# A planned two-layer encoder kernel: library pauses counted for GpSimd, an early broadcast from xT, another order of steps in the feed-forward groups, and a last half stored in three cuts

## The chip, the cores and the metric

The kernel runs on one core of a Trainium2 chip. The time is the device time of one execution in microseconds; the profiled execution's span (first to last instruction) is given beside it. The engines are TensorE (PE, with PEld for its weight loads), VectorE (DVE), ScalarE (ACT), GpSimd (POOL) and SyncE (SP), which issues most of the loads.

## The reference

Two layers on x of 256 tokens by 1024, in float32. Each layer has three steps with a residual and a LayerNorm: half of a gated feed-forward, a mixer, and half of a second gated feed-forward. The mixer of layer 0 is a bidirectional chunked mLSTM, that of layer 1 is attention in a window of 128 tokens.

```python
def swiglu(x, w_in, w_out):                      # 1024 -> 2 x 2816 -> 1024
    gu = x @ w_in
    g, u = gu[..., :D_FF], gu[..., D_FF:]
    return (jax.nn.silu(g) * u) @ w_out

def reference(x, ...):
    for l in range(DEPTH):                       # DEPTH = 2
        x = layer_norm(ALPHA * x + 0.5 * swiglu(x, ffn_w_in[l, 0], ffn_w_out[l, 0]), ...)
        y = mlstm_mixer(x, ...) if l % 2 == 0 else window_attention(x, ...)
        x = layer_norm(ALPHA * x + y, ...)
        x = layer_norm(ALPHA * x + 0.5 * swiglu(x, ffn_w_in[l, 1], ffn_w_out[l, 1]), ...)
    return x
```

In the mLSTM mixer, q, k, v, an output gate o and the gates i and f come from x @ w_in. For each of four heads and both directions the scores q k^T are multiplied by weights exp(u_s - max) with a causal mask, applied to v and divided by their sum; the two directions are added, each head is normalised, scaled by norm_g, multiplied by sigmoid(o), and goes through w_out.

## The kernel before

**Numbers.** TensorE multiplies in a short float32 format. Each operand is split into a high part and the remainder, and each product is three matmuls (hi·hi, hi·lo, lo·hi; `mm3`, L691). For a block of weights, ScalarE casts the high part `w_hi` and VectorE subtracts to get `w_lo` (`split`, L652); one such block, 512 KB, is called a word here. The tokens are two halves of 128, t = 0 and 1; x stands transposed in the constant tiles `xT_hi` and `xT_lo` (128 x 8 x 256).

**Stages.** There are six: feed-forward, mLSTM, feed-forward, feed-forward, attention, feed-forward. The up-projections and the v part of the mLSTM's projection are made in groups of seven block products in place of eight (`strassen`, L904): P1, P2, S1, S2, S3, S4 and A22, each in two steps. The S products use sums of blocks of x, and some words are sums of blocks of weights: either VectorE adds two loaded words in place (`plus`, rows `b11<-b11,b12`), or a DMA on GpSimd's queue adds one block onto another as it lands (`bring`, L923). A22 takes the word b11 after such an adding DMA (`fourth_word`, L945). In a feed-forward group, T0 and T1 are the transposes of the hidden values of a half, and d is one row of the down-projection (12 matmuls). The order of a group is a string: FIRST, FULL, SHUT and OPEN (L54 to 57) for the feed-forward, used 1, 11, 4 and 3 times, and MIXES for the mLSTM. In the mLSTM, H0 to H3 make a head's scores and weights, M0 to M3 the mix with v, the division and the head's normalisation.

**The planner.** Nothing is issued where it is written. `Book` records every instruction, `cost` (L333) gives each a duration, `latest` (L396) a due time counted back from TensorE's order, and `sequence` (L424) simulates the five engines and picks for each the next instruction among those due first. TensorE's order alone is the written one. `emit` then issues all of them, so that every instruction of the kernel has line 600 (611 after the change). The table FEW (L63) holds how long a small DMA on GpSimd's queue is counted to take to land, by the tile that it fills.

**GpSimd's part.** It raises to a power (`TENSOR_TENSOR` with `mhalf`: the reciprocal root of a LayerNorm, `rs`, and of a head's normalisation, `hrs`, L804 and L1373), copies a row to all partitions (`partition_broadcast`, which is a bare ISA row in the program's order), masks (`affine_select`), and issues the adding DMAs. In the mLSTM, `scans` (L1246) makes the gates' running sums and maxima; `most` (128 x 2 x 256) takes the maxima by two small DMAs, and `weights(h)` (L1288) broadcasts head h's row of it into `wt`, ScalarE takes the exponentials, and GpSimd masks them. A broadcast of `gl` into `most` (L1248) is overwritten later: its result is not used.

**The end.** In the last stage's half t = 1 the first step of the LayerNorm (mean and gain) runs on pieces of 512, 256 and 256 columns, the second (power and bias) and the store on the two `cuts` of 512 (`Norm.finish`, L789 to 813).

## Time and profile before

| | |
|---|---|
| three runs | 910.62, 910.65, 911.04 us |
| the profiled execution | 910.77 us |
| its span | 909.1 us |
| mean granted TensorE clock | 0.996 |
| DMA | 220.07 MB, mean 242 GB/s |
| the chain that ended last | PE 73%, issue 10%, DVE 8%, DMA 4%, ACT 3%, POOL 2% |

How to read it: busy time is given for each engine in microseconds and as a share of the span. A row of a timeline is one instruction, or several in a row of one kind (x2), with its start, its duration, the engine, the tiles that it writes and reads, and in brackets how long its engine stood idle before it and which instruction ended that. In the program's order a tile's name carries a number (`b11_1424`), in the timeline it doesn't (`b`).

### The profile page before, as it was taken

The numbers are of one execution on the slowest core, as the hardware profiler recorded it, in microseconds if no ns is written. First come the engines' busy times: TensorE is split into PE (matmuls) and PEld (weight loads), VectorE is DVE, ScalarE is ACT, GpSimd is POOL, SyncE is SP. The second block draws the span as 40 slices with busy tenths as digits, with TensorE's granted clock in tenths as the row PEclk, the third lists the DMA queues.
The fourth block names the chain that finished last, engine by engine and source line by source line (L and its number), as shares of the span: only waits on it lengthen the run. The fifth ranks groups of instructions, "written<-read, shape, count | busy, mean of one in ns | idle before, by whom it ended". The sixth has DMA issues, their size and how long they took to land.

```text
span 909.1 us, 12673 instructions
## 1 busy us (share of the span) xinstructions
PE 892.3 (98%) x4375; PEld 743.6 (82%) x4375; DVE 823.9 (91%) x1008; ACT 656.5 (72%) x927; POOL 169.8 (19%) x201
## 2 busy tenths in 40 slices
PE   8999999999989999999999999999999999999996
PEld 7888888887978888888888888888898788888885
DVE  7999998798987999999889999997789899999974
ACT  6767677685866887776768767775689888677651
POOL 0111221213321212122021212140132231112100
PEclk9999999999999999999999999999999999999999
DMA  9998999937585999999985899999533778999931
GB/s 320 379 305 215 333 300 283 286 75 197 181 277 145 229 236 330 266 267 307 344 238 144 215 319 299 269 268 365 181 123 109 182 188 217 318 256 280 319 71 46
DMA packets 107744, 220.07 MB, mean 242 GB/s; under 512 B 7288, under 2 KB 23696, under 8 KB 107680
## 3 DMA queue, kind: packets, MB, share of 16 engines
q1 hardware_dynamic: 84000, 174.09, 54.6%
q0 software_dynamic: 23680, 45.18, 29.1%
q8 instruction: 34, 0.56, 0.2%
q14 instruction: 30, 0.25, 0.1%
HBM read 218.18 MB, written 1.05 MB: 241 GB/s over the span
## 4 chain that ended last, share of the span: by engine, by line
PE 73%; issue 10%; DVE 8%; DMA 4%; ACT 3%; POOL 2%; DVEq 0%; SPq 0%; POOLq 0%; ACTq 0%
PE pw L600 45%; PE py L600 28%; DVE w_lo L600 3%; DMA b<-in_ffn_w_in_dram 2%; ACT w_hi L600 1%; POOL b L600 1%; DMA b<-in_ml_w_in_dram 1%; DMA raw<-in_ffn_w_in_dram 1%; DVE e L600 0%; DVE pv L600 0%; DMA raw<-in_ffn_w_out_dram 0%; DVE x L600 0%; DVE h L600 0%; ACT sc L600 0%; POOL rs L600 0%
## 5 line engine op out<-in xcount | busy, mean ns | idle before, releaser
L600 ACT CAST w_hi<-b 128x1024 fp32r<-128x1024 f32 x280 | 292.0, 1053 | 107.8 <-PE py L600 48.3
L600 DVE TENSOR_TENSOR w_lo<-b,w_hi 128x1024 fp32r<-128x1024 f32 x280 | 334.4, 1221 | 11.5 <-ACT w_hi L600 10.9
L600 PE MATMUL pw<-w_hi,S 128*128 128x512 f32 x640 | 205.4, 390 | 0.1
L600 DVE TENSOR_TENSOR w_lo<-raw,w_hi 128x1024 fp32r<-128x1024 f32 (+1 forms) x150 | 179.1, 1213 | 11.7 <-ACT w_hi L600 10.9
L600 POOL DMA_DIRECT2D b<-in_ffn_w_in_dram x80 | 97.1, 1225 | 493.5 <-DVE b L600 205.8
L600 ACT CAST w_hi<-raw 128x1024 fp32r<-128x1024 f32 (+1 forms) x150 | 155.0, 1041 | 40.8 <-PE py L600 20.5
L600 PE MATMUL pw<-w_hi,xT_hi 128*128 128x512 f32 (+1 forms) x400 | 157.8, 396 | 1.9 <-ACT w_hi L600 1.2
L600 PE MATMUL pw<-w_hi,xT_lo 128*128 128x512 f32 (+1 forms) x400 | 154.7, 388 | 0.2 <-DVE xT_lo L600 0.2
L600 PE MATMUL pw<-w_lo,xT_hi 128*128 128x512 f32 (+1 forms) x400 | 153.9, 388 | 0.8 <-DVE w_lo L600 0.8
L600 PEld LDWEIGHTS pw<-w_hi,S 128*128 128x128 f32 x640 | 120.1, 188 | 25.8 <-ACT S L600 0.5
L600 PE MATMUL pw<-w_lo,S 128*128 128x512 f32 x320 | 124.5, 389 | 0.0
L600 PE MATMUL py<-w_hi,h_hi 128*128 128x512 f32 x317 | 124.4, 393 | 0.0
L600 PE MATMUL py<-w_hi,h_lo 128*128 128x512 f32 x317 | 123.6, 390 | 0.0
L600 PE MATMUL py<-w_lo,h_hi 128*128 128x512 f32 x317 | 123.4, 389 | 0.0
L600 DVE TENSOR_TENSOR b<-b,b 128x1024 f32<-128x1024 f32 x74 | 90.4, 1223 | 0.8
L600 PEld LDWEIGHTS pw<-w_hi,xT_lo 128*128 128x128 f32 x400 | 75.3, 188 | 17.4 <-DVE xT_lo L600 2.0
L600 PEld LDWEIGHTS pw<-w_hi,xT_hi 128*128 128x128 f32 x400 | 75.3, 189 | 17.3 <-ACT w_hi L600 1.9
L600 PEld LDWEIGHTS pw<-w_lo,xT_hi 128*128 128x128 f32 x400 | 75.4, 189 | 15.3 <-DVE w_lo L600 1.5
L600 PEld LDWEIGHTS pw<-w_lo,S 128*128 128x128 f32 x320 | 60.1, 188 | 12.2
L600 PEld LDWEIGHTS py<-w_hi,h_lo 128*128 128x128 f32 x317 | 59.5, 188 | 12.6
L600 PEld LDWEIGHTS py<-w_lo,h_hi 128*128 128x128 f32 x317 | 59.6, 188 | 12.0
L600 PEld LDWEIGHTS py<-w_hi,h_hi 128*128 128x128 f32 x317 | 59.5, 188 | 12.0
(211 smaller groups left out, 1134.5 us busy)
## 6 DMA issues: line engine op xcount, KB each, us to landing
b<-in_ffn_w_in_dram SPq DMA_DIRECT2D x152, 512.0 KB, 8.0
raw<-in_ffn_w_out_dram SPq DMA_DIRECT2D x88, 512.0 KB, 8.6
b<-in_ffn_w_in_dram POOLq DMA_DIRECT2D x80, 512.0 KB, 9.2
raw<-in_ffn_w_in_dram SPq DMA_DIRECT2D x36, 256.0 KB, 6.6
raw<-in_ml_w_in_dram SPq DMA_DIRECT2D x16, 512.0 KB, 6.0
raw<-in_at_w_in_dram SPq DMA_DIRECT2D x12, 512.0 KB, 8.9
b<-in_ml_w_in_dram SPq DMA_DIRECT2D x8, 512.0 KB, 6.6
raw<-in_ml_w_out_dram SPq DMA_DIRECT2D x8, 512.0 KB, 3.5
```

The costliest lines, as they stand in the source:

```text
L600: getattr(engines[s.engine], s.name)(*[real(x) for x in s.args], **{k: real(x) for k, x in s.kw.items()})
```

## The change

It has five parts. The planner keeps which of two libraries GpSimd has loaded ("B" for `partition_broadcast`, "A" for the rest, with `affine_select` and DMAs belonging to either) and counts 7200 ns (SWITCH) when the next instruction needs the other one. Some of its numbers for GpSimd change: FEW for `most`, and the costs of the broadcast, the select and the power of more than one column. A new broadcast of 8 columns of `xT` into a small tile `ready`, which nothing reads, stands ahead of the gates, and the broadcast of `gl` is gone. In FULL, SHUT and OPEN single steps stand elsewhere. The last half's final cut of 512 columns becomes two of 256, each with its scaling and its store.

```diff
-FULL = "P1*2 d T1 P2*2 S1*2 S2*2 d S3*2 S4*2 d A22*2 d T0"
-SHUT = "T1 P1*2 d P2*2 S1*2 S2*2 d*2 S3*2 S4*2 A22*2 T0"
-OPEN = "a*1 P1*2 a*3 p P2*2 x1 b*1 x2 S1 b*1 S1 S2 x3 x4 b*1 S2 b*1 S4*2 t S3*2 d A22*2 T0"
+FULL = "P1*2 d T1 P2*2 S1*2 S2*2 d S3*2 d S4*2 A22*2 d T0"
+SHUT = "T1 P1*2 d P2 d P2 S1*2 S2*2 d S3*2 S4*2 A22*2 T0"
+OPEN = "a*1 P1*2 a*3 p P2*2 x1 b*1 x2 S1 b*1 S1 S2 x3 x4 b*1 S2 S4 b*1 S4 t S3*2 d A22*2 T0"
-FEW = {"most": 8500.0, "few": 9500.0}
+FEW = {"most": 3200.0, "few": 9500.0}
+SWITCH = 7200.0
+    def library(self):
+        return {"partition_broadcast": "B", "affine_select": "", "dma_start": ""}.get(self.name, "A")
-            s.takes = {"tensor_tensor": 1500.0, "partition_broadcast": 1100.0, "iota": 600.0,
-                       "affine_select": 1600.0}.get(s.name, n * 0.93 + 100.0)
+            s.takes = {"tensor_tensor": 1500.0, "partition_broadcast": 900.0, "iota": 600.0,
+                       "affine_select": 900.0}.get(s.name, n * 0.93 + 100.0)
+            if s.name == "tensor_tensor" and n > 1:
+                s.takes = 1000.0
+        library = "A"
-                    if e == "POOL" and "accum_op" not in s.kw:
+                    if e == "POOL" and "accum_op" not in s.kw and s.name != "partition_broadcast":
                         t = max(t, s.due - EARLY)
+                    if e == "POOL" and s.library() not in ("", library):
+                        t = max(t, free[e] + SWITCH)
+            if e == "POOL":
+                library = s.library() or library
-            cuts = [slice(0, 512), slice(512, D)] if self.last else [A]
+            cuts = [slice(0, 512), slice(512, 768), slice(768, D)] if self.parted else [slice(0, 512), slice(512, D)] if self.last else [A]
         def gates():
+            nc.gpsimd.partition_broadcast(small("ready", (128, 8)), xT[0][0:1, 7, 248:256].bitcast(F32))
         def scans():
             nc.scalar.copy(gl, pg[64:128])
-            nc.gpsimd.partition_broadcast(most[:, 0], gl[0:1])
```

GpSimd's order at the start of the mLSTM stage before: `rs` is the power of the stage's first LayerNorm, `b11` are the two words of A22 that the adding DMAs complete, and `most` the broadcast's target. A bare ISA row names no tile.

```order
L600 DMA few_74<-in_ml_norm_g_dram 128x8x1
L600 TENSOR_TENSOR rs_1789<-rs_1789,few_74 128x1
L600 DMA b11_1407<-in_ml_w_in_dram 128x2x512
L600 ISA
L600 ISA most_1900<-gl_1896 128x256
L600 DMA b11_1424<-in_ml_w_in_dram 128x2x512
L600 DMA most_1900<-scan_1915 4x256 x2
```

The same place after:

```order
L611 DMA few_74<-in_ml_norm_g_dram 128x8x1
L611 TENSOR_TENSOR rs_1789<-rs_1789,few_74 128x1
L611 ISA
L611 ISA ready_1872<-xT_hi_71 128x8
L611 DMA b11_1405<-in_ml_w_in_dram 128x2x512
L611 DMA b11_1424<-in_ml_w_in_dram 128x2x512
L611 DMA most_2052<-scan_1915 4x256 x2
```

The bare ISA row and a broadcast moved from between the two adding DMAs to a place ahead of both, and the broadcast reads `xT_hi` in place of `gl`.

GpSimd's order at the heads of the mLSTM before: `wt_2355` and `wt_2426` are the weights of heads 2 and 3, the first `hrs` is the power of head 0, the second that of head 1.

```order
L600 ISA wt_2355<-most_1900 128x256 x2
L600 AFFINE_SELECT wt_2355<-wt_2355 128x256 x2
L600 ISA wt_2426<-most_1900 128x256 x2
L600 ISA
L600 TENSOR_TENSOR hrs_2437<-hrs_2437,few_74 128x2
L600 AFFINE_SELECT wt_2426<-wt_2426 128x256 x2
L600 TENSOR_TENSOR hrs_2601<-hrs_2601,few_74 128x2
```

And after, where `wt_2343` and `wt_2398` are the weights of heads 2 and 3:

```order
L611 ISA wt_2343<-most_2052 128x256 x2
L611 AFFINE_SELECT wt_2343<-wt_2343 128x256
L611 ISA wt_2398<-most_2052 128x256
L611 AFFINE_SELECT wt_2343<-wt_2343 128x256
L611 ISA wt_2398<-most_2052 128x256
L611 AFFINE_SELECT wt_2398<-wt_2398 128x256 x2
L611 ISA
L611 TENSOR_TENSOR hrs_2426<-hrs_2426,few_74 128x2
L611 TENSOR_TENSOR hrs_2576<-hrs_2576,few_74 128x2
```

The bare ISA row and head 0's power now stand behind head 3's selects.

VectorE's order there before: `den` is a mix's divisor, `h0` and `h1` are the two token halves of the heads' output, `hmv` and `hrs` a head's mean and power, and `wt` are head 2's weights, which become TensorE's operand `a`.

```order
L600 TENSOR_TENSOR den_2495<-den_2495,ecol_2072 128x4
L600 RECIPROCAL den_2495<-den_2495 128x4
L600 TENSOR_SCALAR h0_2397<-h0_2397,hmv_2433,hrs_2437 128x256
L600 TENSOR_TENSOR wt_2355<-pw_2500,wt_2355 128x2x256
L600 TENSOR_TENSOR wt_2355<-pw_2500,wt_2355 128x2x128
L600 TENSOR_SCALAR h1_2402<-h1_2402,hmv_2433,hrs_2437 128x256
L600 SCALAR_TENSOR_TENSOR h0_2397<-py_2450,den_2495,h0_2397 128x256
L600 TENSOR_TENSOR a_lo_2535<-wt_2355,a_hi_2527 128x768
```

And after; head 0's scaling by `hrs_2426` comes eleven rows behind the last one shown:

```order
L611 TENSOR_TENSOR den_2458<-den_2458,ecol_2073 128x4
L611 RECIPROCAL den_2458<-den_2458 128x4
L611 TENSOR_TENSOR wt_2343<-pw_2502,wt_2343 128x2x256
L611 TENSOR_TENSOR wt_2343<-pw_2502,wt_2343 128x2x128
L611 SCALAR_TENSOR_TENSOR h0_2385<-py_2454,den_2458,h0_2385 128x256
L611 BN_STATS hst_2530<-h0_2385 128x6
L611 BN_AGGR hmv_2534<-hst_2530 128x2
L611 TENSOR_TENSOR a_lo_2538<-wt_2343,a_hi_2526 128x768
```

The scaling that needs head 0's power has moved from ahead of head 2's weights to behind the weights and divisors of heads 2 and 3.

VectorE's order in the last group but one of the last feed-forward stage before: `e2` and `e5` become the hidden values of the two halves, whose transposes T0 and T1 follow, `b11` rows with two `b` are sums of words, and `w_lo` are remainders.

```order
L600 TENSOR_TENSOR e2_8152<-pw_8098,e2_8152 128x512
L600 TENSOR_TENSOR e2_8152<-e1_8109,e2_8152 128x512
L600 TENSOR_TENSOR b11_7946<-b11_7946,b12_8086 128x1024
L600 TENSOR_TENSOR w_lo_8247<-b21_8076,w_hi_8213 128x1024
L600 TENSOR_TENSOR w_lo_8255<-b11_7931,w_hi_8225 128x1024
L600 TENSOR_TENSOR b11_7931<-b11_7931,b22_8114 128x1024
L600 TENSOR_TENSOR e5_8126<-g1_8268,e5_8126 128x512
L600 TENSOR_TENSOR w_lo_8280<-b11_7946,w_hi_8257 128x1024
```

And after:

```order
L611 TENSOR_TENSOR b11_7945<-b11_7945,b12_8114 128x1024
L611 TENSOR_TENSOR w_lo_8236<-raw_8005,w_hi_8224 128x1024
L611 TENSOR_TENSOR e2_8153<-pw_8099,e2_8153 128x512
L611 TENSOR_TENSOR e2_8153<-e1_8110,e2_8153 128x512
L611 TENSOR_TENSOR w_lo_8256<-b21_8087,w_hi_8233 128x1024
L611 TENSOR_TENSOR w_lo_8267<-b11_7932,w_hi_8246 128x1024
L611 TENSOR_TENSOR e5_8127<-g1_8270,e5_8127 128x512
L611 TENSOR_TENSOR b11_7932<-b11_7932,b22_8138 128x1024
```

The step of e5 moved ahead of one addition of words; the steps of e2 moved behind the other addition and a remainder of the down-projection.

## The prediction

> **What bounds the kernel now.** I read the totals first, then the order of time on TensorE, then the queues of the engines that it waits for.
>
> ```profile
> PE 892.3 (98%) x4375; PEld 743.6 (82%) x4375; DVE 823.9 (91%) x1008; ACT 656.5 (72%) x927; POOL 169.8 (19%) x201
> ```
>
> TensorE's busy time is 892.3 of 909.1 us. It reads as nearly full, and the number of matmuls is the same after the change, so what there is to win is its 16.8 us without work and any stretch at a lower clock. Apart from the two ends of the span, the places where it waits lie nearly all in the mLSTM stage. The timeline of TensorE (start, duration, engine, instruction, and in brackets the idle time before it and who ended that) has these places:
>
> ```profile
> 220.97 0.39 PE L600 MATMUL pw<-w_hi,xT_lo 128*128 128x512 f32 x1
> 222.09 0.50 PE L600 MATMUL pw<-w_hi,xT_hi 128*128 128x512 f32 x1 [0.74 <-ACT w_hi L600]
> 223.35 0.50 PE L600 MATMUL pw<-w_lo,xT_hi 128*128 128x512 f32 x1 [0.76 <-DVE w_lo L600]
> ...
> 233.79 0.28 PE L600 MATMUL pw<-q_lo,k_hi 128*128 128x256 f32 x1
> 234.83 0.38 PE L600 MATMUL pw<-q_hi,k_lo 128*128 128x256 f32 x1 [0.76 <-DVE k_lo L600]
> ...
> 242.15 0.28 PE L600 MATMUL py<-v_hi,a_lo 128*128 128x258 f32 x1
> 242.89 0.35 PE L600 MATMUL pw<-xT_hi,w_hi 128*128 128x256 f32 x1 [0.45 <-DVE wt L600]
> ...
> 248.71 0.28 PE L600 MATMUL py<-v_hi,a_hi 128*128 128x258 f32 x1
> 250.85 0.39 PE L600 MATMUL pw<-w_hi,xT_hi 128*128 128x512 f32 x1
> 252.24 0.28 PE L600 MATMUL pw<-q_hi,k_hi 128*128 128x256 f32 x1
> ...
> 256.20 0.39 PE L600 MATMUL pw<-w_hi,xT_lo 128*128 128x512 f32 x1
> 258.62 0.39 PE L600 MATMUL py<-v_hi,a_hi 128*128 128x258 f32 x1 [2.03 <-ACT a_hi L600]
> ...
> 262.30 0.63 PE L600 MATMUL pw<-w_hi,xT_hi 128*128 128x512 f32 x1
> ...
> 264.57 0.28 PE L600 MATMUL py<-v_hi,a_hi 128*128 128x258 f32 x1
> ```
>
> I take a start-to-start distance against the undisturbed one. Six 512-column matmuls take 252.24 - 250.85 = 1.39, or 0.23 each; the 18 of one head's mix take 250.85 - 248.71 = 2.14, or 0.12 each.
> - (a) 220.97 to 223.35 holds two matmuls: 2.38 less 0.46 is **1.9** lost. They wait for the second word of the A22 product, b11.
> - (b) 233.79 to 234.83 holds one of 0.12: **0.9** lost, for k_lo.
> - (c) 242.15 to 242.89, likewise: **0.6**, for head 1's weights wt on VectorE.
> - (d) Head 2's mix: 256.20 to 258.62 is 2.42 for one of 0.23, 2.2 lost. Its 18 take 262.30 - 258.62 = 3.68, so 1.5 more than head 1's, and the six behind it 2.27, so 0.9 more than 1.39. Together **4.6**.
>
> In all 8.0 us. Why the matmuls behind the wait are slow is in the table of stretches (busy time and count of PE, PEld, DVE, ACT, POOL, then the granted clock, the DMA share, GB/s):
>
> ```profile
> 261.00:262.00 1.00, 1.00 (x6) 1.00 (x6) 1.00 (x3) 0.58 (x3) 0.00 (x0) 0.50 0.43 142
> ```
>
> The granted clock is 0.50 there. So the 0.9 and a good part of the 1.5 in (d) are the clock's, and I let them go with the wait.
>
> The page "TensorE: Matmul & The Clock Gate" of the Trainium skill (Part 1) says that the clock drops to half after an idle window of about 3.4 us. The row of (d) has 2.03 us of idle, and the clock dropped all the same; the measurement decides. By the page alone the slow matmuls would have another cause and could stay: 0.9 to 2.4 us of the sum, which would come to 904.9 to 906.4.
>
> **Who makes these waits.** GpSimd's own timeline:
>
> ```profile
> 189.78 1.53 POOL L600 TENSOR_TENSOR rs<-rs,few 128x1 f32<-128x1 f32 x1 [4.71 <-DVE rs L600]
> ...
> 200.05 1.21 POOL L600 DMA_DIRECT2D b<-in_ml_w_in_dram  x1 [8.74 <-DVE w_lo L600]
> 209.48 1.80 POOL L600 PARTITION_BROADCAST most<-gl  x1 [8.22 <-DVE w_lo L600]
> 211.13 1.43 POOL L600 DMA_DIRECT2D b<-in_ml_w_in_dram  x1
> ...
> 247.26 0.96 POOL L600 PARTITION_BROADCAST wt<-most  x2 [1.24 <-issue]
> 255.50 0.73 POOL L600 TENSOR_TENSOR hrs<-hrs,few 128x2 f32<-128x2 f32 x1 [7.27 <-issue]
> 256.21 0.82 POOL L600 TENSOR_SCALAR_AFFINE_SELECT wt<-wt 128x256 f32<-128x256 f32 x2
> ```
>
> Twice it stands still between a power (TENSOR_TENSOR rs, hrs) and a broadcast: 201.26 to 209.48 is **8.2**, and 248.22 to 255.50 is **7.3**. The program's order has a bare ISA row at just these two places, and no wait in between that would last so long. I read these as the pauses that the change counts.
>
> The first pause holds back the DMA at 211.13, the second word of (a). From issue to landing the two adding DMAs at 200.05 and 211.13 took:
>
> ```profile
> DMA to landing us min/median/max: 7.1/7.1/7.1
> ...
> DMA to landing us min/median/max: 9.8/9.8/9.8
> ```
>
> The second landed at 211.13 + 9.8 = 220.9. ScalarE stood for 8.5 us in front of it, and VectorE for 2.6:
>
> ```profile
> 209.73 1.07 ACT L600 CAST w_hi<-b 128x1024 fp32r<-128x1024 f32 x1
> ...
> 220.99 1.05 ACT L600 CAST w_hi<-b 128x1024 fp32r<-128x1024 f32 x1 [8.51 <-DMA b<-in_ml_w_in_dram]
> ...
> 222.07 1.23 DVE L600 TENSOR_TENSOR w_lo<-b,w_hi 128x1024 fp32r<-128x1024 f32 x1 [2.64 <-ACT w_hi L600]
> ```
>
> The second pause delays head 0's power hrs. VectorE's queue holds head 0's scaling h ahead of head 2's weights wt, so that head 2 waits for a power that it doesn't need. The first row is again one of the stretches, with VectorE busy for 4.93 of 5.00, the others are VectorE's timeline:
>
> ```profile
> 245.00:250.00 5.00, 5.00 (x44) 5.00 (x43) 4.93 (x12) 3.63 (x7) 1.99 (x4) 1.00 0.63 216
> ...
> 256.27 0.50 DVE L600 TENSOR_SCALAR h<-h,hmv,hrs 128x256 f32<-128x256 f32 x1 [2.83 <-POOL hrs L600]
> 256.69 1.00 DVE L600 TENSOR_TENSOR wt<-pw,wt 128x512 f32<-128x512 f32 x2
> ```
>
> **The change, part by part.** The sums go against the profiled execution: span 909.1, its time 910.77, 1.7 around the span that I leave as it is; the median is 910.65, 0.1 lower. The numbers of the planner set only an order; no instruction gets faster by them.
>
> *First pause.* It now starts behind the power that ends at 189.78 + 1.53 = 191.31. With 7.3 to 8.2 it ends at 198.6 to 199.5. The new broadcast ready (8 columns) needs the last xT_hi:
>
> ```profile
> 193.93 1.07 ACT L600 CAST xT_hi<-py 128x512 fp32r<-128x512 f32 x2 [0.26 <-PE py L600]
> ```
>
> That is done at 195.0, inside the pause. A broadcast took 0.5 (half of the pair at 247.26) to 1.8 (209.48), so GpSimd is free at 199.1 to 201.3. The first adding DMA goes at 200.05 to 201.3, at most 1.25 late; 7.1 to land makes 208.4, ahead of 209.73 where ScalarE takes it. The second follows 1.2 behind, at 201.3 to 202.5, and lands by 212.3 even with the 9.8 of today; ScalarE is free for it at 220.99 - 8.51 = 212.48. So (a) goes and ScalarE gains up to 8.5. VectorE can take that word right behind its other work, 2.6 earlier. The removed broadcast of gl (1.8) was only in the way. SP's loads now share the transfer engines with this word; no wait of TensorE here is for one of them, and I take nothing for it.
>
> *Second pause.* It now stands behind the last select of head 3, and VectorE's queue has the weights of heads 2 and 3, their remainders a_lo and head 2's division ahead of the scaling that needs the power. So the 2.8 at 256.27 goes, and (d) with it. The power itself comes later than today, though: head 3's selects need ScalarE's exponentials,
>
> ```profile
> 250.33 1.85 ACT L600 ACTIVATE wt<-wt,ucol 128x128 f32<-128x128 f32 x6
> ```
>
> which end at 252.2, or at 248.8 if all comes 3.4 earlier, by (a) to (c). Two selects (0.8, the row at 256.21) and the pause make 256.9 to 257.8, the power (0.73) 257.6 to 258.5. VectorE asks for it after head 2's mix, which ends at 262.30 today and 8.0 earlier, 254.3, at best, and some 2 us of queue after that. It may wait 0 to 2 us there; behind it stand the divisions of heads 2 and 3, and then the transposes of the stage's end. I take 1.
>
> *What is late next.* VectorE, which is full between 222.07 and the wait at 256.27. TensorE can come no earlier than VectorE lets it: its waits of 2.6 and 2.8 make 5.5 us that are free if both go. The upper end is TensorE's own 8.0. (b) and (c) go only as far as VectorE's earlier start reaches. I take **6.3**: TensorE's 8.0, less 1 for the power, less 0.7 of (b) and (c); it is nearer to VectorE's 5.5, as VectorE has no slack of its own. Kept for the range: 5.5 less 2 for the power, 3.5, to 8.0.
>
> *Steps in another order.* FULL, SHUT and OPEN move one down product (12 matmuls) or half a product; no matmul is added. In the last stage VectorE's order also changes:
>
> ```profile
> 855.57 0.60 PE L600 MATMUL pw<-ident,e 128*128 128x128 f32 x4
> 854.84 1.22 DVE L600 TENSOR_TENSOR b<-b,b 128x1024 f32<-128x1024 f32 x1
> 855.98 0.68 DVE L600 TENSOR_TENSOR e<-g,e 128x512 f32<-128x512 f32 x1
> ```
>
> The first four transposes start at 855.57, and four more need e, whose step runs from 855.98 to 856.66: with 0.60 for the first four TensorE stands for half a microsecond. The step of e now stands ahead of the addition at 854.84 (1.1 with its distance to the next), but two steps and a remainder changed places before it, so that I give it only 0.3. I take **0.3**, from 0 to 0.5. Elsewhere in the feed-forward stages TensorE waits for nothing that could go, so the moves can only cost there. VectorE is their cover; if one down's move left an instruction late, it would cost up to one remainder (1.1) per group. I take 0. In one group two adding DMAs also go behind two small GpSimd steps for the attention; TensorE has no wait at their words today, and I take 0.
>
> *Last half stored in two pieces.* The end of the span:
>
> ```profile
> 904.32 1.41 DVE L600 SCALAR_TENSOR_TENSOR x<-x,rs,ln_b 128x512 f32<-128x512 f32 x2
> L600 DVE SCALAR_TENSOR_TENSOR x<-pw,mv,ln_g x2: 477/478/478, 903.5 to 903.9; 128x256 f32<-128x256 f32 x2
> 906.00:906.50 0.50, 0.00 (x0) 0.00 (x0) 0.00 (x0) 0.00 (x0) 0.00 (x0) 0.50 1.03 381
> ```
>
> Today two 512-column steps end at 905.73 and two stores of 256 KB follow. Three steps end 0.1 later: a 256-column one takes 478 against 748, and there is one more. The last store is 128 KB instead of 256; at 381 GB/s that is 0.3 shorter. **0.2** is won, between 0.3 lost (the third store's issue, whose price I set at the time that 128 KB takes to move, not hidden, and nothing gained) and 0.4 won.
>
> Sum: 6.3 + 0.3 + 0.2 = 6.8; 910.77 - 6.8 = **904.0**.
>
> **The rivals.**
> - *The load begins only at the first use.* Both pauses end at an instruction whose input came early in the pause, so the rows can't tell a load that starts at the ISA row from one that starts when the broadcast may go. Then the new pause runs from 195.0 to 203.2 and ready ends at 203.7 to 205.0; the first adding DMA goes then and lands 7.1 later, at 210.8 to 212.1, 1.1 to 2.4 behind 209.73. ScalarE's exponentials for the gates stand behind that word, and TensorE takes their result at once:
>
> ```profile
> 217.65 0.33 PE L600 MATMUL pw<-ident,scan 64*128 64x64 f32 x2
> ```
>
> So 1.1 to 2.4, say 1.8, comes back: **905.8**. The page "GPSIMD Engine Reference" (2.1) of the Trainium skill prices the first call of a fresh library at about 6 us after the event wait, which speaks for this reading; the rows say 7.3 and 8.2, and with 6 the pause would end at 201.0, the DMA land by 209.9 and 0.2 at most be lost, which is the forecast again.
> - *VectorE keeps head 2 waiting.* TensorE comes earlier by (a) to (c), VectorE doesn't, and the wait of (d) stays with its half clock. Then 3.4 + 0.5 is won: **906.9**. For it: VectorE has no slack in the stretches ahead. Against it: its wait of 2.8 at 256.27 has lost its cause, and is longer than TensorE's 2.2.
> - *The pauses don't go where the plan puts them.* Another power lands between the broadcasts or the loads pay elsewhere: **910.5**. The built order speaks against it: one ISA row ahead of ready and one behind the last select.
> - *Slower.* The down moved one place in FULL and SHUT makes VectorE late once in each of 11 + 4 groups. At 0.6 each, half of one remainder, that is 9 us: 910.8 - 6.8 + 9 = **913**. It decides from 6.8 / 15 = 0.45 us per group. For it: VectorE is busy for 91% of the span. Against: each product keeps its neighbours of at least one down or product.
>
> **How the numbers follow.** Forecast 0.55; first use 0.17; VectorE 0.14; no effect 0.08; slower 0.06. 904.0 is the likeliest case's. By the bounds it reaches from 8.0 + 0.5 + 0.4 won, 901.9, to 3.5 + 0 - 0.3 won, 907.6. The ends of all terms at once are rare; with the next two cases inside and the last two (0.14) left out I give 902.2 to 907.5. A measurement of this kernel can tell about 0.2%, 1.8 us, from no change: faster 0.86 (the first three), same 0.08, slower 0.06.
>
> **What would show it.** In the trace after: GpSimd idle for 7 to 8 us ahead of ready and not ahead of a DMA of b11; the second such DMA issued at about 202; no wait of ScalarE from 212 to 221; head 2's mix without a drop of the granted clock; a second pause that ends before VectorE asks for hrs. If TensorE waits at the transposes of ig and scan, the first rival holds. If its rate between 300 and 640 drops in each group, the last does. The prediction is wrong above all if something that I took as covered by VectorE's early start, the remainders of q and k, isn't.

## The result, and the profile after

| | before | changed |
|---|---|---|
| median | 910.63 us (909.45 to 911.04, 4 runs) | 903.30 us (902.56 to 904.21, 4 runs) |
| ratio of the runs | | 0.9922, 95% interval 0.9905 to 0.9939 |
| profiled execution, span | 910.77, 909.1 | 903.07, 901.3 |

The change wins 7.3 us of the median; by the interval 5.6 to 8.7. The profiled executions differ by 7.7, their spans by 7.8.

The page of the changed kernel, its totals and the shares of the chain that ended last:

```profile
PE 889.7 (99%) x4375; PEld 742.4 (82%) x4375; DVE 823.1 (91%) x1009; ACT 657.2 (73%) x927; POOL 174.2 (19%) x201
...
PE 87%; issue 4%; DVE 3%; DMA 2%; ACT 2%; POOL 1%; SPq 0%; DVEq 0%; POOLq 0%; ACTq 0%
```

There are as many matmuls as before. The chain runs through TensorE for 87% where it was 73. The shares that shrank most are "issue", time in which the engine on the chain waited for nothing that the profile shows (4% for 10), and VectorE (3% for 8).

GpSimd's timeline of the changed kernel (start, duration, engine, instruction, and in brackets the idle time before it and who ended that):

```profile
189.64 1.54 POOL L611 TENSOR_TENSOR rs<-rs,few 128x1 f32<-128x1 f32 x1 [4.70 <-DVE rs L611]
196.69 0.28 POOL L611 PARTITION_BROADCAST ready<-xT_hi  x1 [5.52 <-ACT sg L611]
199.68 1.37 POOL L611 DMA_DIRECT2D b<-in_ml_w_in_dram  x1 [2.70 <-DVE w_lo L611]
201.65 1.20 POOL L611 DMA_DIRECT2D b<-in_ml_w_in_dram  x1 [0.60 <-ACT gl L611]
...
246.27 0.41 POOL L611 TENSOR_SCALAR_AFFINE_SELECT wt<-wt 128x256 f32<-128x256 f32 x1 [1.17 <-ACT wt L611]
255.81 2.15 POOL L611 TENSOR_TENSOR hrs<-hrs,few 128x2 f32<-128x2 f32 x2 [9.13 <-DVE a_lo L611]
```

The first pause lies between the power and ready, 191.18 to 196.69, 5.5 us. The two adding DMAs follow, and the one that was issued at 211.13 goes at 201.65. The second pause lies behind the last select, 246.68 to 255.81, 9.1 us. Next, what waited for it: ScalarE's cast of the second word of the A22 product (before: at 220.99 after 8.51 of idle), VectorE's scaling of head 0 (before: 2.83 of idle, with head 2's weights behind it), and TensorE's timeline at heads 2 and 3.

```profile
212.29 1.04 ACT L611 CAST w_hi<-b 128x1024 fp32r<-128x1024 f32 x1
```
```profile
257.19 0.74 DVE L611 TENSOR_SCALAR h<-h,hmv,hrs 128x256 f32<-128x256 f32 x2 [0.35 <-POOL hrs L611]
```
```profile
251.90 0.39 PE L611 MATMUL pw<-w_hi,xT_lo 128*128 128x512 f32 x1
252.13 0.28 PE L611 MATMUL py<-v_hi,a_hi 128*128 128x258 f32 x1
...
254.41 0.39 PE L611 MATMUL pw<-w_hi,xT_hi 128*128 128x512 f32 x1
...
256.77 0.28 PE L611 MATMUL py<-v_hi,a_lo 128*128 128x258 f32 x1
257.46 0.39 PE L611 MATMUL py<-v_hi,a_hi 128*128 128x258 f32 x1 [0.42 <-ACT h L611]
```

The cast has no idle time in front of it. Head 2's mix follows the matmul ahead of it at 0.23, and its 18 matmuls take 254.41 - 252.13 = 2.28, where the same took 3.68. A new wait of 0.42 stands in head 3's mix. The stretch from 252 to 264 runs at full clock (busy times and counts of PE, PEld, DVE, ACT, POOL, then the granted clock, DMA share, GB/s):

```profile
252.00:264.00 12.00, 11.58 (x68) 10.13 (x67) 11.07 (x34) 7.19 (x19) 3.62 (x4) 1.00 1.06 362
```

The end of the span, by VectorE's timeline and by the rows of tile x:

```profile
896.46 1.53 DVE L611 SCALAR_TENSOR_TENSOR x<-x,rs,ln_b 128x512 f32<-128x512 f32 x3
```
```profile
L611 SPq DMA_DIRECT2D out_dram<-x x5: 332/347/398, 890.4 to 898.1; - x5
...
DMA to landing us min/median/max: 2.0/2.0/2.1
```

Three scalings take 1.53 where two took 1.41, and each store needs from issue to landing the 2.0 us that it needed before, whatever its size.

To compare the traces I read three stretches of each: M from the transposes of ig, in the mLSTM stage, to the first matmul with S in the next stage, the rest from there up to the end of the last matmul, and the tail up to the span's end. The three rows of the changed kernel:

```profile
217.17 0.33 PE L611 MATMUL pw<-ident,ig 64*128 64x64 f32 x2
...
303.55 0.47 PE L611 MATMUL pw<-w_hi,S 128*128 128x512 f32 x1
...
893.89 0.28 PE L611 MATMUL pw<-w_hi,h_lo 128*128 128x256 f32 x1
```

M is 303.55 - 217.17 = 86.4, the rest 893.89 + 0.28 - 303.55 = 590.6, the tail 901.3 - 894.17 = 7.1. Before, read in the same way, they are 94.0, 590.8 and 7.1. In these two traces 7.6 of the 7.8 us are in M, which is the mLSTM stage from its gates on and the first part of the next.

### The profile page after: what moved, and what is told of

Its sections match the earlier page's. It is cut to its first block, busy times and chain, and to the rows that moved or that the text cites. A ratio compares the mean times of both kernels' runs of the same rounds, so it can differ in the third digit from the quotient of the medians.

```text
span 901.3 us, 12669 instructions
## 1 busy us (share of the span) xinstructions
PE 889.7 (99%) x4375; PEld 742.4 (82%) x4375; DVE 823.1 (91%) x1009; ACT 657.2 (73%) x927; POOL 174.2 (19%) x201
## 3 DMA queue, kind: packets, MB, share of 16 engines
HBM read 218.18 MB, written 1.05 MB: 243 GB/s over the span
## 4 chain that ended last, share of the span: by engine, by line
PE 87%; issue 4%; DVE 3%; DMA 2%; ACT 2%; POOL 1%; SPq 0%; DVEq 0%; POOLq 0%; ACTq 0%
PE pw L611 56%; PE py L611 32%; DMA b<-in_ffn_w_in_dram 1%; DMA raw<-in_ffn_w_in_dram 1%; ACT w_hi L611 1%; POOL b L611 1%; DVE w_lo L611 0%; DVE x L611 0%; DVE pv L611 0%; ACT sc L611 0%; POOL rs L611 0%; DVE pr L611 0%; DMA x<-in_x_dram 0%; ACT pr L611 0%; DVE sc L611 0%
## 5 line engine op out<-in xcount | busy, mean ns | idle before, releaser
L611 DVE TENSOR_TENSOR w_lo<-b,w_hi 128x1024 fp32r<-128x1024 f32 x280 | 334.1, 1218 | 11.0 <-ACT w_hi L611 10.4
```

Of the source, the lines that this page charges most:

```text
L611: getattr(engines[s.engine], s.name)(*[real(x) for x in s.args], **{k: real(x) for k, x in s.kw.items()})
```

## The experiments

All are compared with the kernel before, which ran 909.8 to 909.9 in the median beside them (908.1 to 913.0), somewhat less than in the first runs. The last three columns are the profiled execution's own M, rest and tail. The stretch ahead of M is not in the table: it lasts 216.6 to 217.6 us in nine of the traces, but 218.6 in e1_orders and 218.8 in e5_planner, and these two are late already at 58 us.

| run | median | ratio, 95% interval | M | rest | tail |
|---|---|---|---|---|---|
| before (first profile) | 910.63 | | 94.0 | 590.8 | 7.07 |
| e1_orders | 910.00 | 0.9998 (0.9988 to 1.0008) | 93.0 | 590.9 | 7.04 |
| e2_store | 910.51 | 0.9998 (0.9987 to 1.0010) | 92.1 | 591.0 | 7.20 |
| e4_ready | 906.35 | 0.9958 (0.9946 to 0.9969) | 89.9 | 591.2 | 7.01 |
| e8_second_only | 907.53 | 0.9971 (0.9960 to 0.9982) | 91.2 | 590.7 | 6.98 |
| e5_planner | 904.83 | 0.9931 (0.9913 to 0.9950) | 87.1 | 591.3 | 6.97 |
| e6_planner_ready | 903.35 | 0.9922 (0.9910 to 0.9934) | 86.4 | 591.6 | 6.99 |
| changed (first profile) | 903.30 | 0.9922 (0.9905 to 0.9939) | 86.4 | 590.6 | 7.13 |
| c_after (changed, again) | 902.89 | 0.9926 (0.9911 to 0.9941) | 88.0 | 589.6 | 7.17 |
| e7_switch9 | 902.41 | 0.9911 (0.9893 to 0.9930) | 86.7 | 590.4 | 7.14 |
| e9_two_prices | 901.94 | 0.9913 (0.9898 to 0.9928) | 86.3 | 590.0 | 7.19 |

### One pause, the other, both

The theory is that of the prediction: each pause holds up its own waits of TensorE. Its main rival has VectorE's own waits as the measure. The four kernels none, first, second and both tell them apart.

**The first pause alone**, on the kernel before:

```diff
         def gates():
+            nc.gpsimd.partition_broadcast(small("ready", (128, 8)), xT[0][0:1, 7, 248:256].bitcast(F32))
...
-            nc.gpsimd.partition_broadcast(most[:, 0], gl[0:1])
```

> The kernel before with one edit: the small broadcast ready ahead of the gates, and the broadcast of gl gone. In the built order the first pause moves ahead of both adding DMAs, the second stays between head 3's broadcasts and its selects. Theory A (each pause holds up its own waits of TensorE, and the two add): the losses (a), (b) and (c) go, 3.4 us, and (d) stays with its half clock: 910.6 - 3.4 = 907.2. Theory B (VectorE's two waits are what is won, 2.6 and 2.8): 910.6 - 2.6 = 908.0, and VectorE's wait for head 0's power stays near 2.8. Theory C (the early broadcast does it all, the planner's numbers nothing): 903.3. If the library is loaded only once the broadcast may go, the pause ends at about 203 and the adding DMA is issued behind that; if it is loaded at the bare ISA row, the broadcast comes at about 197, as in the changed kernel.

The ratio makes 3.8 us (2.8 to 4.9): theory A's 3.4 lies in it, B's 2.6 just outside, C's 7 far out. Of the waits (a) and (b) nothing is left in TensorE's timeline; of (c) 0.28 is. (d) stands as before. Its rows, in the timelines of GpSimd and of TensorE and in the table of stretches:

```profile
196.28 0.28 POOL L600 PARTITION_BROADCAST ready<-xT_hi  x1 [5.69 <-ACT sg L600]
...
250.84 0.73 POOL L600 TENSOR_TENSOR hrs<-hrs,few 128x2 f32<-128x2 f32 x1 [6.99 <-issue]
```
```profile
253.96 0.39 PE L600 MATMUL py<-v_hi,a_hi 128*128 128x258 f32 x1 [1.75 <-ACT a_hi L600]
...
254.96 0.58 PE L600 MATMUL py<-v_hi,a_lo 128*128 128x258 f32 x1 [0.49 <-DVE a_lo L600]
```
```profile
254.00:255.00 1.00, 0.51 (x3) 0.30 (x3) 1.00 (x2) 1.00 (x3) 0.00 (x0) 0.79 1.02 324
255.00:258.00 3.00, 3.00 (x14) 3.00 (x15) 2.83 (x7) 1.50 (x4) 0.00 (x0) 0.50 0.78 282
```

ready comes at 196.28, as early as in the changed kernel. The second pause is 7.0, TensorE waits 1.75 and 0.49 for head 2, and the clock falls to 0.50 behind it: 0.42 of the first microsecond shown, since 0.79 is its mean, and the next three, 3.4 us in all.

**The second pause alone**: the planner's new numbers, with the broadcast of gl as before and the switch counted only on the way back to a power.

```diff
-                    if e == "POOL" and s.library() not in ("", library):
+                    if e == "POOL" and s.library() not in ("", "B", library):
                         t = max(t, free[e] + SWITCH)
```

> The planner's new numbers with the old order strings, the old cuts and the broadcast of gl as before, and with SWITCH counted only for the way back from a broadcast to a power. In the built order the first pause stays between the two adding DMAs, the second stands behind head 3's selects. Theory A: (d) goes, 4.6, and (a) to (c) stay, so about 906.0, with ScalarE's wait of 8.5 for the second word and no stretch at half clock behind 250. Theory B: 910.6 - 2.8 = 907.8. Theory C: 910.6.

2.6 us (1.6 to 3.6). That is B's number, but not B's reason. (a) and (b) stay, as A says, (c) is gone, where A had it stay, and (d) is gone with its wait and its half clock. What A missed is a wait that comes in its place:

```profile
249.31 0.41 POOL L611 TENSOR_SCALAR_AFFINE_SELECT wt<-wt 128x256 f32<-128x256 f32 x1 [1.14 <-ACT wt L611]
260.75 1.54 POOL L611 TENSOR_TENSOR hrs<-hrs,few 128x2 f32<-128x2 f32 x2 [11.02 <-DVE den L611]
```
```profile
261.51 0.73 DVE L611 TENSOR_SCALAR h<-h,hmv,hrs 128x256 f32<-128x256 f32 x2 [1.60 <-POOL hrs L611]
```
```profile
260.54 0.39 PE L611 MATMUL py<-v_hi,a_hi 128*128 128x258 f32 x1 [0.43 <-ACT h L611]
...
262.69 0.50 PE L611 MATMUL pw<-w_hi,xT_hi 128*128 128x512 f32 x1 [0.82 <-DVE h L611]
```

The pause lasts 11.0 here and ends at 260.75. VectorE now waits 1.60 for head 0's power, the divisions of heads 2 and 3 stand behind that wait, and TensorE waits 0.82 for VectorE's step on h, and in smaller pieces at the stage's end. So (d)'s removal is in part given back. This kernel and the next also have the planner's other new numbers, FEW and the costs; no run has SWITCH without them or them without SWITCH.

**Both**: the changed kernel with the old order strings and the old cuts.

```diff
-FULL = "P1*2 d T1 P2*2 S1*2 S2*2 d S3*2 d S4*2 A22*2 d T0"
+FULL = "P1*2 d T1 P2*2 S1*2 S2*2 d S3*2 S4*2 d A22*2 d T0"
...
-            cuts = [slice(0, 512), slice(512, 768), slice(768, D)] if self.parted else [slice(0, 512), slice(512, D)] if self.last else [A]
+            cuts = [slice(0, 512), slice(512, D)] if self.last else [A]
```

> The changed kernel with the old FULL, SHUT and OPEN and the old two cuts of the last half: the planner and the broadcasts alone. If the gain lies in the mLSTM stage, as theories A and B have it: 903.5, within 0.5 of the changed kernel. If the order strings or the store carry part of it, 1 us or more above the changed kernel.

903.35, the changed kernel's own time. The planner and the broadcasts carry the gain: 7.1 us by the ratio, against 3.8 and 2.6 for the first and the second pause alone; the intervals allow a plain sum. In M, against a mean of 93.0 in the three traces with the old mLSTM order (94.0, 93.0, 92.1), the first alone wins 3.2 (89.9), the second 1.8 (91.2), both 6.7 (86.4). With the first pause out of the way, GpSimd comes to the second one 3 us sooner (246.68 in the changed kernel, 249.72 in e8_second_only), and in the changed kernel's first trace the power is nearly in time for VectorE. But that the two win more than their sum is not shown: two traces of the changed kernel differ in M by 1.6 (86.4 and 88.0, c_after below), and in the second of them VectorE waits 1.89 for the power in spite of the earlier start.

**Both without the early broadcast**: as e6_planner_ready, with the broadcast of gl in place of ready.

```diff
-            nc.gpsimd.partition_broadcast(small("ready", (128, 8)), xT[0][0:1, 7, 248:256].bitcast(F32))
...
             nc.scalar.copy(gl, pg[64:128])
+            nc.gpsimd.partition_broadcast(most[:, 0], gl[0:1])
```

> The planner's new numbers without the broadcast ready: the broadcast of gl stays, old order strings, old cuts. In the built order the first pause now stands behind both adding DMAs and ahead of the small DMAs of scan into most, the second behind head 3's selects. If the second adding DMA's place is what counts, and not the early broadcast: 903.5, as with ready; the pause then runs from about 203 to 211, before the small DMAs are asked for at 217. If the early broadcast matters by itself (a pause among the transfers that is longer, or that makes the small DMAs late): 905 or more.

Between the two expectations, and the interval overlaps that of e6_planner_ready, so the times don't settle it. GpSimd's timeline shows what happens:

```profile
203.31 1.20 POOL L611 DMA_DIRECT2D b<-in_ml_w_in_dram  x1 [0.53 <-DVE w_lo L611]
214.93 0.97 POOL L611 PARTITION_BROADCAST most<-gl  x1 [10.42 <-DVE scan L611]
```

The pause behind the DMAs lasts 10.4 and still ends ahead of the small DMAs, as expected. So what matters is that the second adding DMA goes ahead of the pause, or the pause ahead of both: either place does. e7_switch9, below, says the same: there the pause ahead of ready stands behind both DMAs, and its time (902.41) and its M (86.7) are as good as the changed kernel's. What the early broadcast is worth by itself stays open. M differs by 0.8 (87.1 and 86.4, before rounding), less than two traces of one kernel do, and the profiled execution of e5_planner had lost 2.1 us against that of e6_planner_ready by 58 us, long before the edited place.

### The parts that don't touch the mLSTM stage

**The order strings alone**, on the kernel before (FULL, SHUT and OPEN as in the change):

```diff
-FULL = "P1*2 d T1 P2*2 S1*2 S2*2 d S3*2 S4*2 d A22*2 d T0"
+FULL = "P1*2 d T1 P2*2 S1*2 S2*2 d S3*2 d S4*2 A22*2 d T0"
...
```

> The kernel before with the new FULL, SHUT and OPEN alone. The changed kernel's trace has TensorE 0.2 us ahead outside the mLSTM stage, from about 0.9 won in the last stage and 0.8 lost in pieces of 0.2: so 910.4, and at most 0.5 away from the kernel before. The slower rival of the prediction (VectorE late once per group) gives 913 or more; a gain in the feed-forward stages that the trace hides gives 909 or less.

No change that the runs can tell, and nothing of the slower rival. The pieces of 0.2 in that expectation were none: they lay at the borders of the stretches in which I had read the timeline. TensorE's wait of 0.56 for e, at 856.73 before, is gone. In this trace a new one has come, at the first matmul with S in the last stage's opening:

```profile
781.28 0.50 PE L600 MATMUL pw<-w_hi,S 128*128 128x512 f32 x1 [0.81 <-ACT e L600]
```

In the six traces with the old strings the column rest has a mean of 591.1 (590.7 to 591.6), in the five with the new ones 590.3 (589.6 to 590.9). That is 0.8 in favour of the new strings, with traces that scatter by 0.4. The one pair that differs in nothing else, before and e1_orders, has none of it (590.8 and 590.9), and the times don't show it either: a gain by the strings is possible and not shown.

**The store alone**:

```diff
-            cuts = [slice(0, 512), slice(512, D)] if self.last else [A]
+            cuts = [slice(0, 512), slice(512, 768), slice(768, D)] if self.parted else [slice(0, 512), slice(512, D)] if self.last else [A]
```

> The kernel before with the last half's three cuts alone. By the prediction's term 0.2 less: 910.4, by the changed kernel's trace (last matmul to the end of the span 7.1 us in both) no change: 910.6. Both lie within what the runs can tell, so the trace decides: the time from the last matmul to the end of the span, 7.07 before, 6.87 by the prediction, 7.1 by the changed trace.

The tail is 7.20. All five traces with three cuts have 7.13 to 7.20, all six with two 6.97 to 7.07. So the third piece costs 0.15 and wins nothing.

This trace has a second reading. Its mLSTM order is that of before, head 2 waits in the same way, and the clock does not fall:

```profile
257.47 0.39 PE L600 MATMUL py<-v_hi,a_hi 128*128 128x258 f32 x1 [1.65 <-ACT a_hi L600]
...
258.47 0.39 PE L600 MATMUL py<-v_hi,a_lo 128*128 128x258 f32 x1 [0.49 <-DVE a_lo L600]
```
```profile
257.00:265.00 8.00, 7.04 (x47) 6.40 (x47) 7.71 (x22) 5.15 (x16) 1.65 (x1) 1.00 0.90 301
```

Of the four traces with this wait, three (before, e1_orders, e4_ready) fall to 0.50, and this one stays at 1.00. Its M is 1.9 shorter than that of before, 0.4 of it by the shorter wait (1.65 for 2.03). Head 2's mix and the six matmuls behind it, 24 in all, take 261.91 - 257.47 = 4.44 here, and 5.95, 5.77 and 5.74 in the three traces with the fall, so that a fall costs 1.3 to 1.5 us.

Why the clock falls in three and not in the fourth can be read from the times of its falls. Behind the last matmul it falls in each of the four. The two falls are at 260.78 and 905.90 in before, at 259.70 and 904.82 in e1_orders, at 254.59 and 899.71 in e4_ready: 645.12 us apart each time. The stretch at half clock lasts 3.41 us, and 645.12 is 189 times 3.413. The program doesn't set this distance: the falls come 0.6 to 2.2 us behind the end of the wait, and 2.0 to 3.9 behind the last matmul. So in these traces the clock is decided at the borders of a grid of 3.41 us. In e2_store the fall behind the last matmul is at 902.28; 645.12 earlier, at 257.16, is such a border, and it cuts the wait in two (TensorE stands from 255.82 to 257.47). By the table of stretches TensorE is busy for 2.07 us of the window ahead of that border and 2.61 of the one behind it, against 1.67, 1.74 and 1.55 in the windows ahead of the three falls. Where the limit lies is not shown: one window of e6_planner_ready, over the end of the last matmuls, had 1.60 and brought no fall.

### The pause by itself

Two kernels that run only powers and broadcasts on GpSimd, with or without loads beside them.

```python
turns(3)                                  # a power, then two broadcasts of a loaded row
power()
nc.vector.tensor_scalar(late[:, 0:4], p, 1.0, None, op0=OP.mult)
for _ in range(10):                       # the broadcast's input comes late
    nc.vector.tensor_scalar(late, late, 1.0, None, op0=OP.mult)
nc.gpsimd.partition_broadcast(wide[0], late[0:1, 0:256])
...
for j in range(96):                       # 512 KB each, into 16 tiles in turn
    nc.sync.dma_start(words[j % 16]...)
turns(4)
```

> A kernel that leaves out the whole computation and measures the pause by itself: powers and broadcasts in turn on GpSimd, first with no transfers, then once with the broadcast's input made late by eleven steps of VectorE behind the power, then beside 96 loads of 512 KB. The rows so far have the pause at 5.4 with a DMA share of 0.00, 7.1 with 0.55, 8.1 with 0.85 and 9.1 with 0.91. If the transfers lengthen it: 5 to 6 us in the quiet turns and 8 to 9.5 in the loaded ones, in both directions. If the length goes with something else (the direction, the engines beside it): no difference between quiet and loaded. If the load starts at the bare ISA row: the late broadcast follows its input within 1 us; if only when the input is there: about 5.5 behind it.

GpSimd's timeline: two rows of the quiet part, the late broadcast, and four of the loaded part; then VectorE's, whose last step is that broadcast's input.

```profile
23.77 0.98 POOL L35 PARTITION_BROADCAST wide<-x  x2 [5.80 <-issue]
31.62 1.05 POOL L32 TENSOR_TENSOR p<-p,half 128x4 f32<-128x4 f32 x1 [6.87 <-issue]
...
55.32 0.55 POOL L50 PARTITION_BROADCAST wide<-late  x1 [7.71 <-DVE late L49]
...
75.63 0.98 POOL L35 PARTITION_BROADCAST wide<-x  x2 [10.85 <-issue]
87.11 1.05 POOL L32 TENSOR_TENSOR p<-p,half 128x4 f32<-128x4 f32 x1 [10.51 <-issue]
...
129.42 0.98 POOL L35 PARTITION_BROADCAST wide<-x  x2 [6.34 <-issue]
137.87 1.05 POOL L32 TENSOR_TENSOR p<-p,half 128x4 f32<-128x4 f32 x1 [7.47 <-issue]
```
```profile
47.86 7.25 DVE L49 TENSOR_SCALAR late<-late 128x1024 f32<-128x1024 f32 x10
```

With no transfers the pause is 5.8 ahead of a broadcast and 6.9 ahead of a power. The late broadcast starts at 55.32, 0.2 behind its input (47.86 + 7.25 = 55.11): the load doesn't wait for the input, it runs beside it. Beside the loads the pause is 10.9 and 10.5 at first, but 6.3 and 7.5 later, with the same share of the transfer engines (1.05). The 8 to 9.5 that was expected lies between. So the transfers lengthen the pause, but their share alone isn't the measure.

The second kernel has three loaded stretches, the first and third reading the same eight words again and again, the second 48 different ones:

```python
k = j % 8 if same else j
r, c = 256 * (k % 4), 512 * (k // 4 % 10)
```

> Like the first kernel for the pause alone (the whole computation is left out), with three loaded stretches of 48 words of 512 KB and five turns each: the first and the third read the same eight words again and again, the second 48 different words. In the first kernel the loaded pauses fell from 10.8 to 6.3 although the DMA share stayed at 1.05. If it is the onset of the traffic that makes the pause long: 10 to 11 at the start of each stretch and 6 to 7.5 at its end, in all three. If it is what the loads read: the first and third alike from start to end, the second different. If it is neither: the three stretches differ without either pattern, and the cause stays open.

The first broadcast behind a pause in each stretch, and the last one whose pause still lies beside the loads:

```profile
45.94 0.98 POOL L35 PARTITION_BROADCAST wide<-x  x2 [11.15 <-issue]
...
97.97 0.98 POOL L35 PARTITION_BROADCAST wide<-x  x2 [6.20 <-issue]
...
134.61 0.98 POOL L35 PARTITION_BROADCAST wide<-x  x2 [11.31 <-issue]
...
184.33 0.98 POOL L35 PARTITION_BROADCAST wide<-x  x2 [6.30 <-issue]
...
219.91 0.98 POOL L35 PARTITION_BROADCAST wide<-x  x2 [10.42 <-issue]
...
273.03 0.98 POOL L35 PARTITION_BROADCAST wide<-x  x2 [6.46 <-issue]
```

All three start at 10.4 to 11.3 and end at 6.2 to 6.5, with the loads at 361 to 368 GB/s in the first pause and at 387 after it. The length goes with the time since the transfers began, not with what they read; why the pause shortens again under an even load stays open.

### The price in the plan

**SWITCH at 9200**, nearer to the second pause of the first trace:

```diff
-SWITCH = 7200.0
+SWITCH = 9200.0
```

> The changed kernel with SWITCH at 9200 ns in place of 7200, which is nearer to the second pause of the changed trace (9.1). In the built order the first pause with ready stands behind both adding DMAs. If the remaining waits of TensorE behind the second pause (0.57 at head 3's mix, 0.58 and 0.71 at the stage's end) come from the pause being longer than counted: 0.5 to 1 less than the changed kernel, 902.5. If they come from VectorE's own queue: 903.3, no change.

902.41, with an interval that holds both expectations. In the trace the pause behind head 3's selects lasts 11.5, the first pause lies among the loads (9.5), and M is 86.7: no gain there against the 86.4 of the changed kernel's first trace.

**The changed kernel again, and with two prices**, on one chip:

> The changed kernel again, on the same chip as the next run: 903.3, and in its trace the second pause again 9 us or more, with VectorE's wait for head 0's power between 0.3 and 1.6 and TensorE's waits of 0.6 behind it.

The same program has a second pause of 11.3 in this trace, 2.2 more than in the first:

```profile
257.58 1.54 POOL L611 TENSOR_TENSOR hrs<-hrs,few 128x2 f32<-128x2 f32 x2 [11.30 <-issue]
```
```profile
258.35 0.73 DVE L611 TENSOR_SCALAR h<-h,hmv,hrs 128x256 f32<-128x256 f32 x2 [1.89 <-POOL hrs L611]
```
```profile
257.08 0.40 PE L611 MATMUL py<-v_hi,a_hi 128*128 128x258 f32 x1 [0.44 <-ACT h L611]
...
259.53 0.50 PE L611 MATMUL pw<-w_hi,xT_hi 128*128 128x512 f32 x1 [1.08 <-DVE h L611]
```

VectorE waits 1.89 for the power, more than the 0.3 to 1.6 that was expected, and TensorE 1.08 behind that. The 0.44 ahead of it is for ScalarE, as in the first trace.

```diff
-SWITCH = 7200.0
+SWITCH = {"B": 5600.0, "A": 10500.0}
...
-                        t = max(t, free[e] + SWITCH)
+                        t = max(t, free[e] + SWITCH[s.library()])
```

> The changed kernel with two prices for the pause in place of 7200 ns for both: 5600 ahead of a broadcast and 10500 ahead of a power, as the traces have them. TensorE's order is unchanged; in the built order VectorE's scaling of head 0's half h0 stands eight rows later, behind head 2's division and head 3's divisor. If the prediction's term for the power (1 us, kept as a loss) is real and sits in VectorE's wait for it: that wait goes, TensorE's wait of 0.57 at head 3's mix goes, and the time is 0.5 to 1 under the changed kernel, 902.5. If VectorE's queue behind that point is what TensorE waits for: the wait only moves to the transposes of the stage's end, and the time stays at 903.3.

901.94 in six runs of 901.26 to 902.28, against 902.89 in six of 902.24 to 904.92. The 0.9 is 0.1%, and the intervals of the two ratios overlap, so the times don't settle it. What the trace shows:

```profile
257.88 2.12 POOL L611 TENSOR_TENSOR hrs<-hrs,few 128x2 f32<-128x2 f32 x3 [11.72 <-DVE h L611]
```
```profile
256.91 0.88 DVE L611 SCALAR_TENSOR_TENSOR h<-py,den,h 128x256 f32<-128x256 f32 x2 [0.60 <-ACT h L611]
```
```profile
256.93 0.39 PE L611 MATMUL py<-v_hi,a_hi 128*128 128x258 f32 x1 [0.44 <-ACT h L611]
```

The pause is 11.7, longer than in c_after, and VectorE has nothing that waits for it: the 1.08 is gone. Against c_after M is 1.7 shorter (86.3 for 88.0), against the changed kernel's first trace, where the pause was 9.1, it is the same. The 0.44 for ScalarE stays, so that one never was the power's; there the expectation was wrong. This version has the lowest median of all kernels here, but not by more than the runs scatter.

## Why the prediction was right

- **The place of the gain.** Right. 6.3 was put on the mLSTM stage; M gives 7.6 between the two first profiles, and 5.8 between the means of the three traces with the old mLSTM order (93.0) and of the two of the changed kernel (87.2). e6_planner_ready has the whole gain without strings and store.
- **The first pause.** Right, and shorter than said: 5.5 for 7.3 to 8.2. The second adding DMA was to go at 201.3 to 202.5 and went at 201.65; the first went at 199.68, held by VectorE's remainder of the word, no longer by the pause. (a), (b) and (c) are all gone from the changed trace. The 0.7 kept back for (b) and (c) was not lost: that term was mis-sized.
- **The rival that the load begins only at first use.** It fell: the broadcast ready starts 1.8 behind its input (the two casts of xT_hi end at 194.87), far less than a load, and in m1_pause a broadcast follows its late input by 0.2.
- **The second pause.** The mechanism was right and a size was off. The pause was taken as 7.3 to 8.2; it is 9.1 and 11.3 in two traces of the same program. The loss of 1 for the power, with 0 to 2 as its range, covers both: VectorE waits 0.35 in one and 1.89 in the other. e8_second_only and c_after show how thin that cover is: where the pause lasts 11, VectorE's wait and TensorE's behind it come back in part, and the move of the second pause alone won 2.6 where (d) was priced at 4.6.
- **The clock's part of (d).** It was let go with the wait as a sure gain, 0.9 and part of 1.5. The size is right: a fall costs 1.3 to 1.5. The wait is gone and no half clock stands in the changed trace ahead of the last matmul, but e2_store has the old order without the fall. So it is a gain against some executions of the kernel before only. The page "TensorE: Matmul & The Clock Gate" of the Trainium skill (Part 1) calls the window over which the clock is decided free-running and gives its length as about 3.4 us. The grid of 3.41 us in these traces agrees with both. The same part of the Trainium skill has the clock fall after an idle window; here windows in which TensorE was idle for 1.7 to 1.9 of the 3.41 us were enough.
- **VectorE keeps head 2 waiting** fell: head 2's mix starts without a wait. **No effect** fell. **Slower** fell: the strings cost nothing (0.9998, 0.9988 to 1.0008), and if they do anything they win.
- **The strings.** 0.3 was taken, from 0 to 0.5. The wait for e went as said, but no gain is shown: the column rest has 0.8 between the means, and nothing between before and e1_orders.
- **The store.** Wrong in sign: 0.2 won was forecast, 0.15 is lost. The step that failed is "128 KB instead of 256; at 381 GB/s that is 0.3 shorter": from issue to landing both sizes take 2.0, so only the longer scaling is left.

The sum of 6.8 stands against 7.3 in the medians, 5.6 to 8.7 by the interval. Between the two first profiles the terms are 7.6 in M for 6.3, 0.1 in the rest for the strings' 0.3, and 0.1 lost in the tail for 0.2 won. That M came out larger is what was kept back: the 0.7 of (b) and (c), and most of the 1 for the power, which in this trace cost VectorE only 0.35. That the sum is so near is in part luck. Whether the clock falls in an execution of the kernel before, and how long the second pause lasts in one of the changed kernel, each move a single execution by more than 1 us.

## What to carry to other kernels

A pause that no instruction owns is found in the idle time between two operations of different kinds that wait for nothing; what it costs is the queue behind it, so put it where the queue behind it is empty. Ahead of the transfers it is also shorter (5.5 us, against 9.5 and 10.4 among them), though in e7_switch9 the longer one delayed nothing either. Count it in a plan at the length that it has at that place, since with one price for both directions VectorE still waited, 0.35 and 1.89 us in two traces. A store that is cut finer must be paid by the store's own time: where that time is the same for both sizes, the cut only adds an instruction.

## What the runs showed of the hardware

- GpSimd's pause on a change of library is 5.5 to 6.2 us ahead of a broadcast and 6.8 to 7.4 ahead of a power with no transfers beside it. Among the kernel's loads it was 6.7 to 11.7, at the onset of steady loads 10.4 to 11.3, and some 60 us later, at 387 GB/s, 6.2 to 6.5 ahead of a broadcast. The page "GPSIMD Engine Reference" of the Trainium skill (2.1) has about 6 us for the first call of freshly loaded code and says that new code can be brought by DMA. The quiet pauses ahead of a broadcast agree with the first, those ahead of a power are longer; the second could explain the long ones, but no run here shows the code's transfer.
- The load runs while the instruction behind it still waits for its input (0.2 us behind the input in m1_pause).
- TensorE's granted clock falls to 0.50 at the borders of a grid of 3.41 us (falls 645.12 us apart in three traces, 189 steps). Waits of 1.48 to 2.03 us with one of 0.49 behind them brought a fall in three traces; one of 1.65 with the same 0.49, with a border in its middle, brought none (e2_store). A fall lasted 3.41 us and cost 1.3 to 1.5 us.
- A store's time from issue to landing was 2.0 to 2.1 us for 128 KB and for 256 KB.
